# Where the rounded weights of a projection's first tile are kept, in a hybrid decoder step

## The chip, the cores and the metric

The kernel runs on one core of one Trainium2 chip. The metric is the device time of one execution in microseconds (us), the median over the runs shown.

## The reference, cut to what matters

One decoder layer works on 520 token columns (512 prompt positions and 8 samples) of width 1024. It opens and closes with half a gated feed-forward network; between the two stand a convolution group and an attention group with their projections.

```python
def half_ffn(x, g, w1, w3, w2):            # w1, w3: 1024 x 2816, w2: 2816 x 1024
    h = rmsnorm(x, g)
    return x + 0.5 * ((jax.nn.silu(h @ w1) * (h @ w3)) @ w2)

def trunk_layer(x, ffn1, mixw, ffn2, past):
    x = half_ffn(x, *ffn1)
    ...                                     # norm, w_in, convolution and attention, w_out
    x = half_ffn(x, *ffn2)
```

`h @ w1` and `h @ w3` are called the first projection here, and the product with `w2` the second projection.

## The kernel before

**Numbers in two parts.** Every float32 matrix is split into a rounded part `hi` (type float32r) and a rest `lo`. One product is three matmuls (`mm3`, lines 121 to 123): `hi` with the rounded activations, `hi` with their rest, `lo` with the rounded activations. Each has a 128x128 block of weights and 260 columns, half of the tokens. For the weights, `load_w` loads a block into a buffer `raw` (a ring of 4), ScalarE rounds it to `hi` (line 108), and VectorE subtracts to get `lo` (line 109). `hi` and `lo` come from two rings of 3 buffers with the tags `whi` and `wlo`.

**The feed-forward network** (`ffn`, run twice) cuts the 2816 hidden rows into 22 blocks of 128, and these into three stages by `CUTS = (0, 4, 14, 22)`. A stage makes its hidden blocks `hh`, `hl` and then calls `down`, which multiplies them with the rows of `w2` that belong to them and adds the result to `X`, in 8 tiles `m` of 128 output rows. The first stage makes its blocks one at a time. The second and the third make theirs two at a time (`pair`), each pair with two calls of `seven`, one for `w1` (results `a`) and one for `w3` (results `b`). `seven` gets four block products from seven products of half the depth (12 matmuls each) with sums of weights. Its operands are the two loaded weights `ha`, `hb` (with `la`, `lb`), which take two buffers each of the rings `whi` and `wlo`, and the three sums `hs`, `ls`, tiles of 12 blocks in a pool `su` with 2 buffers for each of the tags `hs` and `ls`. Their rounding is on lines 387 to 390. Lines 396 to 409 are the seven products, each followed by its copy or addition out of PSUM. In one accumulator (`px`) a later product goes on only after the copy of the earlier one (lines 397, 401, 405). A pair's last product is the seventh of `w3`; lines 330 and 334 to 338 then make the second hidden block of the pair out of it.

**The second projection.** `down` works on `k1 - k0` hidden blocks: 10 in the second stage, whose weights for one tile come as two loads of 5 blocks, and 8 in the third, one load of 8 blocks. A tile takes one PSUM buffer; `gemm` runs over the two halves of the columns and in each over the hidden blocks.

**Order.** The program order gives priorities. A planner with a timing model turns it, when the kernel is built, into a fixed order for each engine: an instruction whose operands the planner takes for ready can be put ahead of an earlier one that is not. On the chip each engine works through its list in that order. Loads are issued on the queue of SP in the order of their lists too.

**The transitions.** The text calls the passage from the pairs to `down` in the second stage the *first transition*, and in the third stage the *second transition*; there is one of each in both networks, four in all. At a transition the ring `whi` goes like this: the last pair's `w1` has two buffers; its `w3` takes the third for `ha`, and for `hb` the buffer that `ha` of `w1` gives back. The loads of `down` follow: the next buffer is free when the last product with `hb` of `w1` is done, the one after it when the product with `ha` of `w3` is done, and the third only when the pair's last product is done.

Of the kernel before, what the change touches and what calls it, by code (L numbers as in the profile page):

```python
# [8 lines left out]
F32R = mybir.dt.float32r  # L9
# [4 lines left out]
P = 128  # L14
# [6 lines left out]
KD = D // P  # L21
KF = DFF // P
# [16 lines left out]
CUTS = (0, 4, 14, 22)  # L39
# [7 lines left out]
def halves(t):  # L47
    return t.rearrange("p (h n) -> p h n", h=2)
# [3 lines left out]
def tile_step(ctx: ExitStack, tc: tile.TileContext, xT, w0, w1a, w3a, w2a, w_in, w_out, w1b, w3b, w2b,  # L52
# [6 lines left out]
    wp = ctx.enter_context(tc.tile_pool(name="wp", bufs=3))  # L59
# [13 lines left out]
    def preload():  # L73

        tc.keep_in_program_order(A.preload_act_table_set("natural_log_exp_and_others"))
# [4 lines left out]
    def PE_last():  # L80
        return [i for i in nc.cur_bb.bb.instructions if i.engine == mybir.EngineType.PE][-1]

    def keep_warm(n, ps):

        for _ in range(n):
            PE.matmul(ps[:, :P], lhsT=ones, rhs=ones, start=True, stop=True)
# [5 lines left out]
    loads = [0]  # L92
    EVERY = 5

    def load_w(src, n, cuts=None, then=None):
        raw = wp.tile([P, n, P], F32, name="raw", tag="raw", bufs=4)
        hi = wp.tile([P, n, P], F32R, name="hi", tag="whi")
        lo = wp.tile([P, n, P], F32R, name="lo", tag="wlo")
        if cuts:
            for c in cuts:  # L100
                SP.dma_start(raw[:, c], src[:, c])
                V.tensor_copy(hi[:, c], raw[:, c])
                V.tensor_tensor(lo[:, c], raw[:, c], hi[:, c].bitcast(F32), ALU.subtract)
                if c is cuts[0]:
                    then()
            return hi, lo
        load(raw, src)
        A.activation(hi, raw, AF.Copy)  # L108
        V.tensor_tensor(lo, raw, hi.bitcast(F32), ALU.subtract)  # L109
        return hi, lo  # L110

    def load(raw, src):
        d = SP.dma_start(raw, src)
        loads[0] += 1
        if side and loads[0] > 8 and loads[0] % EVERY == 0:
            with tc.issue_after(d.ins):
                side.pop(0)()
# [7 lines left out]
    def gemm(ps, parts, xh, xl, hs=(0, 1), of=None):  # L125

        ks = [(hi[:, i], lo[:, i], k0 + i) for hi, lo, k0, n in parts for i in range(n)]
        for h in hs:
            c = slice(h * TH, (h + 1) * TH)
            for i in range(*(of or (0, len(ks)))):  # L130
                hi, lo, k = ks[i]
                mm3(ps[:, h, :TH], hi, lo, xh[k][:, c], xl[k][:, c], i == 0, i == len(ks) - 1)
# [92 lines left out]
    def ffn(i, w1, w3, w2, g, psum, finish=None):  # L225
        turn, more = [0], []

        def psum_tile():
            turn[0] += 1
            pools = [(p, "m4") for p in more] + [(psM, "mm"), (psM, "mm"), (psum, "m3")]  # L230
            pool, tag = pools[(turn[0] - 1) % len(pools)]
            return pool.tile([P, 2, 512], F32, name="ps", tag=tag)

        Hh, Hl = [None] * KF, [None] * KF

        def hidden(m):
            at = m - max(c for c in CUTS if c <= m)
            pool = hids[at >= CUTS[1]]
            Hh[m] = pool.tile([P, T], F32R, name=f"hh{at}", tag=f"hh{at}")
            Hl[m] = pool.tile([P, T], F32R, name=f"hl{at}", tag=f"hl{at}")  # L240
            return Hh[m], Hl[m]

        with ExitStack() as st, ExitStack() as sx:
# [4 lines left out]
            with tc.tile_pool(name=f"xa{i}", bufs=1, side="right", reuse_waits="tile") as xa, \  # L248
# [23 lines left out]
                if early:  # L272

                    early, ws = [psum_tile() for _ in range(3)], early
                    for k in range(KD):
                        for e, ps in enumerate(early):
                            hi, lo = (t[:, 3 * (k % 2) + e] for t in ws[k // 2])
# [8 lines left out]
                for m in range(CUTS[1]):  # L286
# [3 lines left out]
                    for w, t in ((w1, a), (w3, b)):  # L290
# [5 lines left out]
                        hi, lo = load_w(w[m], KD)  # L296
# [19 lines left out]
            su = sx.enter_context(tc.tile_pool(name=f"su{i}", bufs=2, side="right", reuse_waits="tile"))  # L316

            def pair(m):

                at, aw, bt = psum_tile(), psum_tile(), psum_tile()  # L320
                a = gu.tile([P, 4, TH], F32, name="a", tag="a", bufs=2)
                b = gu.tile([P, 4, TH], F32, name="b", tag="b")
                x = seven(su, w1, m, xs, at, aw[:, 0, :TH], a)
                A.activation(a[:, 0:2], a[:, 0:2], AF.Silu)
                A.activation(a[:, 3], a[:, 3], AF.Silu, scale=-1.0)
                A.activation(a[:, 2], x, AF.Silu, scale=-1.0)
                x = seven(su, w3, m, xs, bt, aw[:, 1, :TH], b)
                V.tensor_tensor(b[:, 0:2], b[:, 0:2], a[:, 0:2], ALU.mult)
                V.tensor_tensor(b[:, 3], b[:, 3], a[:, 3], ALU.mult)
                V.tensor_tensor(b[:, 2], x, a[:, 2], ALU.mult)  # L330
                for r, sign in ((0, 1.0), (1, -1.0)):
                    hh, hl = (halves(t) for t in hidden(m + r))
                    of = b[:, 2 * r:2 * r + 2]
                    A.activation(hh, of, AF.Copy, scale=sign)
                    if r:
                        V.scalar_tensor_tensor(hl, of, sign, hh.bitcast(F32), ALU.mult, ALU.subtract)
                    else:
                        V.tensor_tensor(hl, of, hh.bitcast(F32), ALU.subtract)

            for c0, c1 in zip(CUTS[1:], CUTS[2:]):  # L340
                for m in range(c0, c1, 2):
                    pair(m)
                if c1 < KF:
                    down(w2, c0, c1, Hh, Hl, psum_tile)
            preload()
            sx.close()
            more.clear()
            down(w2, CUTS[-2], KF, Hh, Hl, psum_tile, finish)

    def x_sums(pool, tmp, name, col, k):  # L350

# [57 lines left out]
        V.tensor_tensor(out[:, 1], pw, out[:, 1], ALU.add)  # L409
        return px  # L410

    def down(w2, k0, k1, Hh, Hl, psum_tile, finish=None, ms=range(KD)):

        n = k1 - k0 if k1 - k0 <= KD else (k1 - k0) // 2

        def parts(m):
            return [load_w(w2[m, :, k:k + n], n) + (k, n) for k in range(k0, k1, n)]

        def update(m, ps, h):
            c = slice(h * TH, (h + 1) * TH)  # L420
            V.scalar_tensor_tensor(X[m][:, c], ps[:, h, :TH], 0.5, X[m][:, c], ALU.mult, ALU.add)

        def whole(m):
            ws = parts(m)
            ps = psum_tile()
            gemm(ps, ws, Hh, Hl)
            V.scalar_tensor_tensor(halves(X[m]), ps[:, :, :TH], 0.5, halves(X[m]), ALU.mult, ALU.add)
            if finish:
                finish(m, None)

        for m in ms[:-2] if finish else ms:
            whole(m)
        if not finish:
            return
        ws = [parts(m) for m in range(KD - 2, KD)]
        for h in range(2):
            for m in range(KD - 2, KD - 1):
                ps = psum_tile()
                gemm(ps, ws[m - KD + 2], Hh, Hl, [h])
                update(m, ps, h)  # L440
                finish(m, h)
            ps = psum_tile()
            if not h:
                gemm(ps, ws[-1], Hh, Hl, [0])
                update(KD - 1, ps, 0)
                give = finish(KD - 1, 0)
                continue
            gemm(ps, ws[-1], Hh, Hl, [1], (0, SPLIT))
            with tc.issue_after(tc.keep_in_program_order(give()).ins):
                gemm(ps, ws[-1], Hh, Hl, [1], (SPLIT, k1 - k0))  # L450
            idle = psum_tile()[:, 0]
            with tc.issue_after(PE_last()):
                keep_warm(4, idle)
            update(KD - 1, ps, 1)
            give = finish(KD - 1, 1)
            with tc.issue_after(PE_last()):
                keep_warm(4, idle)
            give()
# [357 lines left out]
    with tc.tile_pool(name="psB", bufs=1, space=PSUM, reuse_waits="tile") as psB, ExitStack() as st_f:  # L816
# [28 lines left out]
        def give(h, ps, r):  # L845

            fp, c = part["p"], slice(h * TH, (h + 1) * TH)
            both = [ps, part["ps"].tile([P, 512], F32, name="nps0", tag="n0")] if h else [ps]
            for p in both:
                mm = spread(p, r, TF, [(t, 0, TF) for t in range(4)])  # L850
            y = fp.tile([P, KD, TH], F32, name="yf", tag=f"yf{h}")
            rs = fp.tile([P, TH], F32, name="rs", tag=f"rs{h}")
            A.activation(rs, both[-1][:, :TH], AF.Copy)
            for ks in ((0,), (1, 2), (3, 4), (6, 7), (5,)):
                for k in ks:
                    if k > 5:
                        G.tensor_tensor(y[:, k], rs, X[k][:, c], ALU.mult)
                    else:
                        V.tensor_tensor(y[:, k], ps[:, :TH], X[k][:, c], ALU.mult)
                ks = slice(ks[0], ks[-1] + 1)  # L860
                SP.dma_start(yT[:, ks, c], y[:, ks])
            return mm

        ffn(1, w1b, w3b, w2b, GV["ffn2"], psB, finish)


# [96 lines left out]
```

## Time and profile before

| what | value |
|---|---|
| runs, median (lowest to highest) | 1001.39 us (1000.5 to 1004.54) |
| profiled execution, its own time | 1001.53 us |
| span of its trace, first to last instruction | 999.7 us |
| mean granted TensorE clock | 0.996 of full speed |

Sums are made against the 1001.53 us of the profiled execution. It lies 0.14 us above the median. The span leaves out 1.83 us of that time, which lie before and after the first and last instruction. The profile lists per engine when each instruction started and how long it took; `PE` is TensorE's matmuls, `PEld` its loads of weights, `DVE` VectorE, `ACT` ScalarE, `SPq` the queue that issues loads. "L108" is line 108 of the kernel.

### The profile page before, as it was taken

To read this page: it belongs to the slowest core of one execution; us is meant where nothing else is said; L and a number is where in the kernel's file an instruction comes from. 1 tells how busy PE (TensorE), PEld (TensorE's weight loads), DVE (VectorE), ACT (ScalarE), POOL (GpSimd) and SP (SyncE) were. 2 spreads that over 40 slices of the span, in tenths; PEclk is the share of its full clock that TensorE was granted. 3 is DMA by queue.
4 is the path that set the end of the run, shared out by engine and by line. 5 is a ranking of instruction groups with operands and counts; after the bars stand their busy time and mean duration, and the time that the engine had idled before them with its cause. 6 is when DMAs were issued, how large, how long until landed. Compare 5 with 4: busy or idle time off the path is not lost.

```text
span 999.7 us, 19200 instructions
## 1 busy us (share of the span) xinstructions
PE 977.4 (98%) x7897; PEld 955.6 (96%) x7897; DVE 719.6 (72%) x1153; ACT 519.9 (52%) x941; POOL 69.7 (7%) x89
## 2 busy tenths in 40 slices
PE   8999999999999999999999999999999999999997
PEld 8999999999999999999999899999999999999997
DVE  7889987336886446667788899769988634788432
ACT  5536665324665446667566555435656422565442
POOL 1000000000000131112022210000000000000022
PEclk9999999999999999999999999999999999999998
DMA  7344343445444444243146565325443233333302
GB/s 243 110 137 164 133 147 123 163 138 173 145 147 130 165 157 149 89 145 138 65 152 228 197 225 191 108 94 179 149 147 127 80 93 104 106 107 106 106 22 86
DMA packets 37912, 136.62 MB, mean 137 GB/s; under 512 B 5760, under 2 KB 8512, under 8 KB 37312
## 3 DMA queue, kind: packets, MB, share of 16 engines
q1 hardware_dynamic: 37824, 135.39, 39.9%
q8 instruction: 62, 1.02, 0.4%
q14 instruction: 26, 0.21, 0.1%
HBM read 131.07 MB, written 37.82 MB: 169 GB/s over the span
## 4 chain that ended last, share of the span: by engine, by line
PE 78%; DVE 11%; DMA 5%; issue 3%; ACT 2%; POOL 1%; SPq 0%; POOLq 0%; DVEq 0%; ACTq 0%
PE ps L121 24%; PE ps L123 24%; PE ps L122 24%; DVE lo L390 2%; DMA raw<-in_w3a 2%; PE s L589 1%; DMA raw<-in_w1a 1%; DVE ls L390 1%; DVE lo L109 1%; DMA raw<-in_w1b 1%; DVE raw L377 1%; PE pt L610 1%; DVE ws L378 1%; DVE ws L376 1%; DVE ws L375 1%
## 5 line engine op out<-in xcount | busy, mean ns | idle before, releaser
L108 ACT ACTIVATE hi<-raw 128x1024 fp32r<-128x1024 f32 (+3 forms) x136 | 119.0, 878 | 208.3 <-PE ps L122 162.7
L121 PE MATMUL ps<-hh,hi 128*128 128x260 f32 x704 | 198.4, 284 | 3.4 <-ACT hi L108 1.4
L123 PE MATMUL ps<-hh,lo 128*128 128x260 f32 x704 | 198.8, 284 | 1.2 <-DVE lo L109 1.2
L122 PE MATMUL ps<-hl,hi 128*128 128x260 f32 x704 | 198.2, 282 | 0.1
L109 DVE TENSOR_TENSOR lo<-raw,hi 128x1024 fp32r<-128x1024 f32 (+3 forms) x136 | 138.6, 1020 | 76.3 <-ACT hi L108 75.0
L121 PEld LDWEIGHTS ps<-hh,hi 128*128 128x128 f32 x704 | 132.3, 189 | 4.9 <-ACT hi L108 1.8
L123 PEld LDWEIGHTS ps<-hh,lo 128*128 128x128 f32 x704 | 132.2, 188 | 2.1 <-DVE lo L109 1.6
L122 PEld LDWEIGHTS ps<-hl,hi 128*128 128x128 f32 x704 | 132.6, 188 | 0.4 <-DVE hl L305 0.3
L121 PE MATMUL ps<-mh,hi 128*128 128x260 f32 x384 | 110.1, 287 | 1.7 <-DVE q L518 1.1
L123 PE MATMUL ps<-mh,lo 128*128 128x260 f32 x384 | 109.4, 285 | 0.2 <-DVE u L643 0.2
L122 PE MATMUL ps<-ml,hi 128*128 128x260 f32 x384 | 109.3, 285 | 0.0
L389 ACT ACTIVATE hi<-raw 128x512 fp32r<-128x512 f32 x144 | 82.9, 622 | 37.2 <-PE ps L122 27.9
L390 DVE TENSOR_TENSOR lo<-raw,hi 128x1024 fp32r<-128x1024 f32 x72 | 87.8, 1219 | 7.2 <-ACT hi L389 6.9
L123 PE MATMUL ps<-f1sh,lo 128*128 128x260 f32 x288 | 81.6, 285 | 1.8 <-DVE lo L390 1.7
L121 PE MATMUL ps<-f0sh,hi 128*128 128x260 f32 x288 | 81.8, 284 | 1.4 <-ACT a L405 1.0
L121 PE MATMUL ps<-f1sh,hi 128*128 128x260 f32 x288 | 81.5, 283 | 0.7 <-ACT a L405 0.5
L123 PE MATMUL ps<-f0sh,lo 128*128 128x260 f32 x288 | 81.3, 285 | 0.7 <-DVE lo L390 0.6
L122 PE MATMUL ps<-f0sl,hi 128*128 128x260 f32 x288 | 81.2, 282 | 0.0
L122 PE MATMUL ps<-f1sl,hi 128*128 128x260 f32 x288 | 81.1, 282 | 0.0
L144 POOL TENSOR_TENSOR acc<-acc,sq 128x520 f32<-128x520 f32 (+1 forms) x19 | 28.9, 1523 | 741.4 <-ACT sq L143 737.5
L121 PEld LDWEIGHTS ps<-mh,hi 128*128 128x128 f32 x384 | 72.4, 189 | 2.8 <-issue 1.8
L122 PEld LDWEIGHTS ps<-ml,hi 128*128 128x128 f32 x384 | 72.4, 188 | 1.1 <-issue 0.7
(278 smaller groups left out, 2664.5 us busy)
## 6 DMA issues: line engine op xcount, KB each, us to landing
out_cko<-in_ck SPq DMA_DIRECT2D x16, 1023.0 KB, 6.8
out_cvo<-in_cv SPq DMA_DIRECT2D x16, 1023.0 KB, 6.8
raw<-in_w_in SPq DMA_DIRECT2D x24, 512.0 KB, 3.3
raw<-in_w1b SPq DMA_DIRECT2D x22, 512.0 KB, 3.3
raw<-in_w3b SPq DMA_DIRECT2D x22, 512.0 KB, 3.3
raw<-in_w3a SPq DMA_DIRECT2D x21, 512.0 KB, 3.3
raw<-in_w1a SPq DMA_DIRECT2D x20, 512.0 KB, 3.3
raw<-in_w2a SPq DMA_DIRECT2D x16, 320.0 KB, 2.9
```

What stands on the lines that cost most here:

```text
L108: A.activation(hi, raw, AF.Copy)
L109: V.tensor_tensor(lo, raw, hi.bitcast(F32), ALU.subtract)
L121: PE.matmul(out, lhsT=hi, rhs=xh, start=start, stop=False, skip_group_check=more)
L122: PE.matmul(out, lhsT=hi, rhs=xl, start=False, stop=False, skip_group_check=more)
L123: PE.matmul(out, lhsT=lo, rhs=xh, start=False, stop=stop, skip_group_check=more)
L144: eng.tensor_tensor(dst[:, c], dst[:, c], sq[:, c], ALU.add)
L375: V.tensor_tensor(s[:, 0], rb[:, :KQ], rb[:, KQ:], ALU.add)
L376: V.tensor_tensor(s[:, 1], s[:, 0], ra[:, :KQ], ALU.add)
L377: V.tensor_tensor(rb[:, :KQ], rb[:, :KQ], ra[:, :KQ], ALU.add)
L378: V.tensor_tensor(s[:, 2], s[:, 1], ra[:, KQ:], ALU.add)
L389: A.activation(h[:, c:c + KQ], f[:, c:c + KQ], AF.Copy)
L390: V.tensor_tensor(l, f, h.bitcast(F32), ALU.subtract)
```

## The change

After the pairs of the second and third stage, the weights of the first tile (`m = 0`) of the second projection are loaded and rounded by a call of their own, and into other buffers: a tile of 12 blocks from the tags `hs` and `ls` of the pool `su` instead of buffers of the rings `whi` and `wlo`. `down` then takes these for `m = 0` and the rings for the other seven tiles. In the third stage the call stands ahead of the load of the activation table (`preload`) and of the closing of the pools; before, the loads of `m = 0` stood behind both.

```diff
-    def load_w(src, n, cuts=None, then=None):
+    def load_w(src, n, cuts=None, then=None, room=None):
         raw = wp.tile([P, n, P], F32, name="raw", tag="raw", bufs=4)
-        hi = wp.tile([P, n, P], F32R, name="hi", tag="whi")
-        lo = wp.tile([P, n, P], F32R, name="lo", tag="wlo")
+        hi, lo = room or (wp.tile([P, n, P], F32R, name=x, tag=f"w{x}") for x in ("hi", "lo"))
...
                 for m in range(c0, c1, 2):
                     pair(m)
+                room = [su.tile([P, 12, P], F32R, name=x, tag=x) for x in ("hs", "ls")]
+                first = down_weights(w2, c0, c1, 0, room)
                 if c1 < KF:
-                    down(w2, c0, c1, Hh, Hl, psum_tile)
+                    down(w2, c0, c1, Hh, Hl, psum_tile, first=first)
             preload()
             sx.close()
             more.clear()
-            down(w2, CUTS[-2], KF, Hh, Hl, psum_tile, finish)
+            down(w2, CUTS[-2], KF, Hh, Hl, psum_tile, finish, first=first)
...
-    def down(w2, k0, k1, Hh, Hl, psum_tile, finish=None, ms=range(KD)):
+    def down_weights(w2, k0, k1, m, room=None):
 
         n = k1 - k0 if k1 - k0 <= KD else (k1 - k0) // 2
+        return [tuple(load_w(w2[m, :, k:k + n], n, room=room and [t[:, k - k0:k - k0 + n] for t in room])) + (k, n)
+                for k in range(k0, k1, n)]
+
+    def down(w2, k0, k1, Hh, Hl, psum_tile, finish=None, ms=range(KD), first=None):
 
         def parts(m):
-            return [load_w(w2[m, :, k:k + n], n) + (k, n) for k in range(k0, k1, n)]
+            return first if first and not m else down_weights(w2, k0, k1, m)
```

## Rows read from the trace of the kernel before

**Rows 1.** The page: the busy time, share of the span and number of instructions of each engine, and the shares of the chain that ended last.

```profile
PE 977.4 (98%) x7897; PEld 955.6 (96%) x7897; DVE 719.6 (72%) x1153; ACT 519.9 (52%) x941; POOL 69.7 (7%) x89
...
PE 78%; DVE 11%; DMA 5%; issue 3%; ACT 2%; POOL 1%; SPq 0%; POOLq 0%; DVEq 0%; ACTq 0%
```

**Rows 2.** The waits of TensorE over the whole span: line waited for, us in total, times, longest.

```profile
PE ps L123 <- DVE lo L109: 2.6, 4, 1.0
...
PE ps L121 <- ACT hi L108: 1.4, 2, 0.7
...
PE ps L121 <- DVE b L330: 1.0, 2, 0.5
```

**Rows 3.** Stretches of the first network: the stretch and its length, then busy us and number of instructions of PE, PEld, DVE, ACT and POOL, the granted TensorE clock, the share of the DMA engines, GB/s. The first two are around and behind the first transition, the third is inside and after the last `down`.

```profile
188.00:196.00 8.00, 7.27 (x57) 6.71 (x56) 3.16 (x5) 2.55 (x4) 0.00 (x0) 1.00 0.15 43
196.00:229.00 33.00, 33.00 (x277) 33.00 (x276) 10.68 (x15) 6.86 (x10) 0.00 (x0) 1.00 0.51 170
...
345.00:385.00 40.00, 40.00 (x336) 40.00 (x335) 19.15 (x27) 16.28 (x23) 10.43 (x8) 1.00 0.40 141
```

**Rows 4.** TensorE's instructions in order of time at the first transition of the first network: start, duration, engine, line, output and inputs, and in brackets the idle time ahead and what ended it. The first row is the end of the pair's last product.

```profile
187.97 0.28 PE L123 MATMUL ps<-f0sh,lo 128*128 128x260 f32 x1
188.96 0.39 PE L121 MATMUL ps<-hh,hi 128*128 128x260 f32 x1 [0.71 <-ACT hi L108]
189.19 0.28 PE L122 MATMUL ps<-hl,hi 128*128 128x260 f32 x1
189.48 0.38 PE L121 MATMUL ps<-hh,hi 128*128 128x260 f32 x1
189.82 0.39 PE L123 MATMUL ps<-hh,lo 128*128 128x260 f32 x1
```

**Rows 5.** ScalarE and VectorE at the same place, in order of time for each: the first three roundings of weights of `down` (line 108), the rounding of the pair's second hidden block (line 334), the rest of the third rounding (line 109) and that of the hidden block (line 336).

```profile
180.43 0.74 ACT L108 ACTIVATE hi<-raw 128x640 fp32r<-128x640 f32 x1 [0.93 <-PE ps L122]
...
181.87 0.74 ACT L108 ACTIVATE hi<-raw 128x640 fp32r<-128x640 f32 x1 [0.43 <-PE ps L122]
...
188.17 0.74 ACT L108 ACTIVATE hi<-raw 128x640 fp32r<-128x640 f32 x1 [2.39 <-PE ps L122]
188.81 0.62 ACT L334 ACTIVATE hh<-b 128x520 fp32r<-128x520 f32 x1
...
188.94 0.83 DVE L109 TENSOR_TENSOR lo<-raw,hi 128x640 fp32r<-128x640 f32 x1 [0.23 <-ACT hi L108]
189.68 0.69 DVE L336 SCALAR_TENSOR_TENSOR hl<-b,hh 128x520 fp32r<-128x520 f32 x1
```

**Rows 6.** TensorE's instructions at the second transition of the first network: three places where the next start is late.

```profile
322.78 0.28 PE L122 MATMUL ps<-hl,hi 128*128 128x260 f32 x1
323.67 0.39 PE L123 MATMUL ps<-hh,lo 128*128 128x260 f32 x1 [0.61 <-DVE lo L109]
...
327.38 0.28 PE L123 MATMUL ps<-hh,lo 128*128 128x260 f32 x1
327.77 0.39 PE L121 MATMUL ps<-f0sh,hi 128*128 128x260 f32 x1
...
329.19 0.28 PE L123 MATMUL ps<-f0sh,lo 128*128 128x260 f32 x1
330.00 0.39 PE L121 MATMUL ps<-hh,hi 128*128 128x260 f32 x1 [0.52 <-DVE b L330]
```

**Rows 7.** ScalarE and VectorE at the second transition: the first rounding of `down` (lines 108 and 109), the copy out of `px` (line 405), the rest of the pair's first hidden block (line 338) and the multiplication that frees the last PSUM buffer of the pair (line 330).

```profile
321.29 1.06 ACT L108 ACTIVATE hi<-raw 128x1024 fp32r<-128x1024 f32 x1 [0.93 <-PE ps L122]
...
327.33 0.39 ACT L405 ACTIVATE b<-ps 128x260 f32<-128x260 f32 x1 [0.97 <-PE ps L123]
...
322.38 1.23 DVE L109 TENSOR_TENSOR lo<-raw,hi 128x1024 fp32r<-128x1024 f32 x1 [1.56 <-ACT hi L108]
...
326.40 0.70 DVE L338 TENSOR_TENSOR hl<-b,hh 128x520 fp32r<-128x520 f32 x1 [0.70 <-ACT hh L334]
...
329.51 0.43 DVE L330 TENSOR_TENSOR b<-ps,a 128x260 f32<-128x260 f32 x1 [0.87 <-PE ps L123]
```

**Rows 8.** TensorE at the two transitions of the second network: the rows that answer to the first two of rows 4 and of rows 6.

```profile
800.69 0.28 PE L123 MATMUL ps<-f1sh,lo 128*128 128x260 f32 x1
801.68 0.39 PE L121 MATMUL ps<-hh,hi 128*128 128x260 f32 x1 [0.71 <-ACT hi L108]
...
934.82 0.28 PE L122 MATMUL ps<-hl,hi 128*128 128x260 f32 x1
935.71 0.39 PE L123 MATMUL ps<-hh,lo 128*128 128x260 f32 x1 [0.61 <-DVE lo L109]
```

**Rows 9.** Inside the last pair ahead of each transition, by start: the loads of `w2` issued ahead of the first transition, the last matmul that reads the sums of `w1` (line 123 with `ls`), then VectorE's rest of `ha` of `w3` (line 390) and the first matmul that reads it; the last two again for the second transition.

```profile
159.30 15.89 SPq L113 DMA_DIRECT2D raw<-in_w2a  x4
...
168.72 0.29 PE L123 MATMUL ps<-f0sh,ls 128*128 128x260 f32 x1
...
171.53 1.23 DVE L390 TENSOR_TENSOR lo<-raw,hi 128x1024 fp32r<-128x1024 f32 x1 [0.63 <-ACT hi L389]
...
173.38 0.28 PE L123 MATMUL ps<-f0sh,lo 128*128 128x260 f32 x1
...
312.40 1.23 DVE L390 TENSOR_TENSOR lo<-raw,hi 128x1024 fp32r<-128x1024 f32 x1 [0.63 <-ACT hi L389]
...
314.25 0.28 PE L123 MATMUL ps<-f0sh,lo 128*128 128x260 f32 x1
```

## The prediction

> **What bounds the kernel now.** The page comes first [rows 1]: TensorE is busy 98% of the span and holds 78% of the chain that ended last; VectorE, at 72%, holds 11%. What counts is then where TensorE waits. In the list of its waits [rows 2] the reader sees that the projection's weights (lines 108 and 109) are behind 1.4 and 2.6 us of idle time, a few waits of under 1 us each, and line 330 behind 1.0 us. The stretches tell where these are not: from 196 to 229 us, inside the second projection, TensorE is busy all 33.00 us [rows 3], 277 matmuls, so 33.00 / 277 = 0.119 us from one start to the next. From 345 to 385 us it is the same, 336 in 40.00 us. From 188 to 196 us there are 57 where 8 / 0.119 = 67 would fit. The gaps belong to the transitions. So the timelines of the transitions come last, and every gap is measured from start to start, less 0.119, because the matmuls overlap.
>
> First transition, first network [rows 4]: after the pair's last product TensorE starts again 0.99 us later, so 0.87 us are lost, and "ACT hi L108" ended them. Then 189.19 to 189.48 and 189.48 to 189.82 lose another 0.17 and 0.22. Together 1.26 us; the ten missing matmuls, 10 x 0.119 = 1.2, say the same. The rounding waited for is the third of `down`: it starts at 188.17 [rows 5], just when the last product has given back the third ring buffer, ends at 188.91, and its rest runs from 188.94 to 189.77, after which line 123 starts at 189.82. The two roundings ahead of it, at 180.43 and 181.87, are tile 0's. Why is there nothing else to do? Tile 0 is held by the pair's second hidden block, whose `hh` is rounded at 188.81 and whose `hl` ends at 189.68 + 0.69 = 190.37; tile 1 has only these late weights.
>
> Second transition [rows 6]: one load is a whole tile, and tile 0's own is the late one. Its rounding starts at 321.29, its rest at 322.38, and ends at 323.61 [rows 7]; line 123 starts at 323.67 instead of 322.90, 0.77 us lost. Two further gaps have other causes: 327.38 to 327.77 (0.27 lost) is the copy of `px` at 327.33, and 329.19 to 330.00 (0.69 lost) is the PSUM buffer of tile 1, which line 330 gives back at 329.94. The second network repeats both transitions [rows 8]: 801.68 - 800.69 = 0.99 and 935.71 - 934.82 = 0.89.
>
> **The change part by part.** No instruction is added or removed. Per network three loads, three roundings and three rests move: tile 0's, two at the first transition and one at the second.
>
> *Ring buffers.* Each load of tiles 1 to 7 now takes a ring place that one of tile 0 had. At the first transition tile 1's two roundings get the places at 180.43 and 181.87, and with rests of 0.83 us each are done before 184, some 5 us ahead of 188.09, when the last product's stream ends. Tile 1 then has two halves, of which the first can run over nine of ten hidden blocks: 9 x 3 = 27 matmuls or 3.2 us, against the 190.37 - 188.09 = 2.3 us until the held block is there. The cover is enough, and the whole 1.26 us go. What now starts at 188.17 is tile 2's first rounding, wanted only after tile 1. Bounds: nothing, if the planner leaves the order as it is and the next wait takes over; 1.26 if all goes.
>
> *The second transition.* Tile 0's weights are ready before 322.65, and the 0.77 us go at their place. What is late next? Tile 0 goes on with the pair's first hidden block, whose `hl` is ready at 326.40 + 0.70 = 327.10 [rows 7] and whose third matmul started at 327.38 [rows 6], so its second at about 327.25: only some 0.15 us earlier are to be had there in the same order. After it the next product waited for the copy at 327.33, which comes earlier with the product it follows; this product can then start at about 327.35 instead of 327.77. Line 330 and tile 1's PSUM buffer follow it, 0.4 us earlier. So I take 0.4 of 0.77; the ends are 0 and 0.77.
>
> *Where the roundings go.* The room is the buffer of the sums of `w1`, whose last reader starts at 168.72 [rows 9], so it is free at 169.0, 11 us ahead of the old place, and the loads are issued from 159.30 on. The roundings then fall among those of the last pair's `w3`. The nearest rows for a price: the rest of `ha` ends at 171.53 + 1.23 = 172.76, and its first reader starts at 173.38; at the second transition 313.63 and 314.25. The slack is 0.62 us both times. One rest of 0.83 us in front costs 0.83 - 0.62 = 0.21, both cost 1.04, one of 1.23 costs 0.61. VectorE had 0.63 us of idle time just ahead of both rows, so part fits in; I take 0.2 us for the kernel as a whole, with bounds of zero and of the second rival's sum.
>
> *Loads, table load, pools.* SP issues the same loads in the same order; tile 0's `raw` come free earlier, and later loads with them. DMA engines are 15 to 51% busy in these stretches [rows 3]. The pools now close with tile 0's sums still in use, but nothing new there is written before tile 0 is added to `X`. I cost these at nothing; their cover is the 40.00 of 40.00 busy us after the second transition. Without it, a load would show as a new wait.
>
> [...]
>
> **Sum.** 2 networks x (1.26 + 0.4) = 3.3, less 0.2, is 3.1 us. 1001.53 - 3.1 = 998.4 us, and against the median, 1001.39, 3.0 us or 0.3% less.
>
> **The rivals.**
>
> *The next wait takes the place of the old.* At the first transition TensorE could run into the held block at 190.37 all the same, if its list keeps tile 0 ahead, or if both loads in one room tile are tracked as one. For it: the list is made with planned times, and in the gap [rows 4] it did not run tile 0's second half, though its weights were there. Against it: it did go on with tile 1, as soon as that had weights. Gain 0 to 1.5 us, time about 1000.6.
>
> *The earlier roundings hold up the last pair.* If the planner puts tile 0's in front of `w3`'s on both engines, then by the durations of their rows [rows 5, 7] the first transition costs 2 x 0.74 + 2 x 0.83 - 0.62 = 2.5 us and the second 1.06 + 1.23 - 0.62 = 1.7; two networks: 8.4, less 3.3: 5.1 us slower, 1006.6. On VectorE alone it is 2 x (1.04 + 0.61) = 3.3, which cancels the gain: 1001.5. So it decides from 0.83 us a transition beyond the slack. For it: the new place has only 0.62 us to spare. Against it: ScalarE is busy 52% and `w3`'s weights come first in the program. [...]
>
> *All gaps of the transitions go,* those of the copy and of line 330 too, since the new list fills them with tile 0's second half: 2 x (1.26 + 0.77 + 0.27 + 0.69) = 6.0, 995.5. Against it: the PSUM buffer is not touched by the change.
>
> *The planner orders other stages otherwise.* Attention has many short steps, whose order comes from the planned times. No row can price it; I give a few us either way, bounded by 5 or so, as much as the largest sum above.
>
> **How the numbers follow.** Chances: forecast 0.55, next wait 0.20, hold-up 0.10, all gaps 0.07, other stages 0.08. The likeliest gives 998.4. The range reaches up past the next wait and the cancelled gain to 1001.8, and down to 995.3, below all gaps gone; it leaves out most of a full hold-up and half of the last case, and some spread of the runs, about 2 in 10. A measurement of this kernel tells about 0.5% (5 us) from no change. Faster by more than that needs all gaps (0.04 of its 0.07), half of the last case (0.03) and 0.02 of the forecast: 0.09. Slower: 0.02 of the hold-up and 0.04 of the last: 0.06. The rest, 0.85, is within.
>
> **What would show it.** Right: no wait "ACT hi L108" over 0.5 us at the first transitions and no "DVE lo L109" at the second ones; three roundings per network on line 108 that start some 9 us earlier among the last pair's; tile 1's matmuls without a pause behind the last product. "DVE b L330" stays as a wait. Wrong: new waits on line 390 or on copies (lines 397 to 405) in the last pair, a pause until the held `hl` behind the last product, or a shift between 400 and 620 us that outweighs the 3 us.

## The result, and the profile after

The changed kernel takes 1014.83 us (median of 4 runs, 1010.43 to 1016.08), the kernel before 1001.39 us beside it (median of 3 runs, 1000.5 to 1004.54). Executions in a slow state, one of the kernel before with 1573.8 us and one in each of the first two experiments, are left out of the medians and ratios here. The ratio of the means is 1.012, with a 95% interval of 1.0096 to 1.0144. The change makes the kernel slower by 1.2%, where 998.4 us, or 0.3% less, had been forecast. The profiled execution took 1013.89 us with a span of 1012.1 us, 12.4 us more than the 999.7 before.

The page after, the line that answers to the first of [rows 1], and below it the groups of ScalarE in which tables of activation functions are loaded (line, engine, operation, count, then busy us and mean ns, and the idle time ahead):

```profile
PE 983.4 (97%) x7897; PEld 960.7 (95%) x7897; DVE 718.6 (71%) x1153; ACT 536.6 (53%) x955; POOL 69.3 (7%) x89
...
L75 ACT ACT_TABLE_LOAD x3 | 3.8, 1283 | 0.8 <-PEq L944 0.7
L182 ACT ACT_TABLE_LOAD x3 | 3.8, 1283 | 0.1
L183 ACT ACT_TABLE_LOAD x3 | 3.8, 1283 | 0.1
L149 ACT ACT_TABLE_LOAD x3 | 3.8, 1283 | 0.1
L150 ACT ACT_TABLE_LOAD x3 | 3.8, 1283 | 0.1
L300 ACT ACT_TABLE_LOAD x2 | 2.6, 1283 | 0.0
L323 ACT ACT_TABLE_LOAD x2 | 2.6, 1283 | 0.0
```

The same groups of the kernel before:

```profile
L75 ACT ACT_TABLE_LOAD x3 | 3.8, 1283 | 0.8 <-PEq L939 0.7
L301 ACT ACT_TABLE_LOAD x2 | 2.6, 1283 | 0.0
```

TensorE, VectorE and GpSimd have the same number of instructions as before [rows 1]; ScalarE has 955 instead of 941. The 14 that were added are table loads of 1.283 us each, 19 against 5. (Line numbers after are one to five off those before: line 107 is the old 108, line 391 the old 390; those of the experiments differ by a few too.) The new ones stand at the logarithms and exponentials of the norms (lines 149, 150, 182, 183) and at the Silu in a pair (line 323).

Where the time went is read from three updates of `X` on VectorE (line 427 or 421 before, 432 or 426 after): the last of the first network, the first of the second, and the last but one of the kernel. Before:

```profile
373.85 0.70 DVE L427 SCALAR_TENSOR_TENSOR X<-ps,X 128x520 f32<-128x520 f32 x1 [2.89 <-PE ps L123]
...
675.75 0.69 DVE L427 SCALAR_TENSOR_TENSOR X<-ps,X 128x520 f32<-128x520 f32 x1
...
984.09 0.43 DVE L421 SCALAR_TENSOR_TENSOR X<-ps,X 128x260 f32<-128x260 f32 x1 [0.31 <-PE ps L123]
```

After:

```profile
374.53 0.70 DVE L432 SCALAR_TENSOR_TENSOR X<-ps,X 128x520 f32<-128x520 f32 x1 [2.89 <-PE ps L122]
...
683.38 0.69 DVE L432 SCALAR_TENSOR_TENSOR X<-ps,X 128x520 f32<-128x520 f32 x1
...
992.23 0.43 DVE L426 SCALAR_TENSOR_TENSOR X<-ps,X 128x260 f32<-128x260 f32 x1 [0.31 <-PE ps L122]
```

The first network, with both of its transitions, costs 0.68 us more. Between the networks another 7.63 - 0.68 = 6.95 us are lost, in the second network 8.14 - 7.63 = 0.51, and behind this update 12.4 - 8.14 = 4.3. So over 11 of the 12.4 us are lost where no line of the change stands. TensorE's three longest waits between 380 and 660 us, first after, then before:

```profile
PE ps L120 <- DVE t L776: 2.8, 2, 2.3
PE ps L120 <- DVE q L523: 1.7, 1, 1.7
PE vt L556 <- DVE v L545: 1.1, 1, 1.1
```

```profile
PE ps L121 <- DVE q L518: 1.1, 1, 1.1
PE ps L121 <- DVE k L518: 0.6, 1, 0.6
PE ps L121 <- DVE t L771: 0.5, 1, 0.5
```

These are the users of the reciprocal roots that the norms deliver. ScalarE after, at the norm behind the first network, shows why they are late:

```profile
384.35 1.28 ACT L182 ACT_TABLE_LOAD   x1
385.65 0.64 ACT L182 ACTIVATE rbc<-rv 128x520 f32<-128x520 f32 x1
...
386.79 1.28 ACT L183 ACT_TABLE_LOAD   x1
388.09 0.64 ACT L183 ACTIVATE rbc<-rbc 128x520 f32<-128x520 f32 x1
```

A load stands ahead of the logarithm (line 182) and another ahead of the exponential (line 183), 2.57 us at one norm. Before, both functions ran at every norm without a load of their own (0 loads on their lines, 3 on line 75, which stand ahead of the norms). The two norms at the end have both loads too. At the last one, the logarithm and the load behind it:

```profile
1001.18 0.21 ACT L149 ACTIVATE rr<-rv 65x4 f32<-65x4 f32 x1
1001.40 1.28 ACT L150 ACT_TABLE_LOAD   x1
```

The waits are not the whole loss. By the full lists TensorE waits 6.7 us from 380 to 660 us after and 2.9 us before, 3.8 us more, where 6.95 us were lost. The rest goes with TensorE's granted clock, which in the changed kernel fell twice in this stretch and in the kernel before not at all. Two stretches of the changed kernel, in the columns of [rows 3]:

```profile
396.00:399.50 3.50, 3.15 (x14) 3.18 (x15) 3.23 (x5) 2.41 (x4) 1.12 (x1) 0.51 0.40 108
611.00:614.50 3.50, 3.50 (x19) 3.50 (x18) 2.18 (x4) 1.20 (x3) 0.00 (x0) 0.51 0.43 150
```

The second again in the kernel *Ring buffers, table load late* (see the experiments), which has the same loads at the norms:

```profile
611.00:614.50 3.50, 3.50 (x32) 3.50 (x31) 3.40 (x7) 2.14 (x4) 0.00 (x0) 1.00 0.47 150
```

At a granted clock of 0.51, 19 matmuls start where 32 start at 1.00; the 13 that are missing are worth 13 x 0.119 = 1.5 us. By the same two updates of `X` (374.18 and 681.72) that kernel, whose clock fell once here, lost 5.64 us, 1.3 us less than the changed kernel. So about 3 of the 6.95 us (an estimate: two falls at 1.3 to 1.5 us) are a lower clock behind the waits. Ahead of the first fall TensorE had waited 1.1 and 1.7 us (for `v` and `q`), ahead of the second 2.3 us (for `t`). The ring-buffer kernel has this last wait too and kept its clock, so why it falls at one place and not at another stays open. At the end of the kernel it was 0.84 from 990 to 1000 us, where the ring-buffer kernel had 1.00 and lost 3.5 us behind the third update instead of 4.3. The mean granted clock was 0.990 or 0.991 in all four runs of the changed kernel, against 0.996 before.

And why do the norms have loads of their own, with line 75's ahead of them? ScalarE before, behind the last pair of the first network, and after, inside that pair:

```profile
330.36 0.62 ACT L334 ACTIVATE hh<-b 128x520 fp32r<-128x520 f32 x1
331.00 1.28 ACT L75 ACT_TABLE_LOAD   x1
```

```profile
310.65 1.06 ACT L107 ACTIVATE hs<-raw 128x1024 fp32r<-128x1024 f32 x1 [2.12 <-PE ps L121]
311.73 1.28 ACT L75 ACT_TABLE_LOAD   x1
313.02 0.39 ACT L402 ACTIVATE a<-ps 128x260 f32<-128x260 f32 x1
...
317.29 1.28 ACT L323 ACT_TABLE_LOAD   x1
318.58 0.64 ACT L323 ACTIVATE a<-a 128x520 f32<-128x520 f32 x1
```

`preload` (line 75) is traced with `keep_in_program_order`. At the transitions shown here the load runs directly behind the one instruction that was traced just ahead of it on ScalarE, wherever the planner put that one. Before, that was the rounding of the pair's second hidden block, the last instruction of the pair there (330.36). After, it is the rounding of tile 0's weights. This runs at 310.65, inside the pair, and the table load follows at 311.73. At 317.29 a load for the pair's own Silu follows, and line 75 has no further load before the norms. At the norm at 384.35 both functions then have loads of their own; before, with line 75's load at 331.00, behind the pair's last Silu, neither has one. So in these runs it goes with the order of the two loads: with the Silu's last the norms have 12 loads (this kernel and *Ring buffers, table load late*), with line 75's last none (the kernel before and *Table load first*). The early load also holds up a copy out of `px` (line 402) for which TensorE waits; its timeline there:

```profile
311.88 0.28 PE L122 MATMUL ps<-f0sh,lo 128*128 128x260 f32 x1
313.46 0.39 PE L120 MATMUL ps<-f0sh,hi 128*128 128x260 f32 x1 [1.29 <-ACT a L402]
```

### The profile page after: what moved, and what is told of

It is laid out like the page before. It is cut to its first block, busy times and chain, and to the rows that moved or that the text cites. A ratio compares the mean times of both kernels' runs of the same rounds, so it can differ in the third digit from the quotient of the medians.

```text
span 1012.1 us, 19208 instructions
## 1 busy us (share of the span) xinstructions
PE 983.4 (97%) x7897; PEld 960.7 (95%) x7897; DVE 718.6 (71%) x1153; ACT 536.6 (53%) x955; POOL 69.3 (7%) x89
## 4 chain that ended last, share of the span: by engine, by line
PE 79%; DVE 9%; DMA 4%; issue 3%; ACT 2%; POOL 1%; SPq 0%; POOLq 0%; DVEq 0%; ACTq 0%
PE ps L120 25%; PE ps L122 25%; PE ps L121 24%; DVE lo L391 2%; PE s L594 1%; DMA raw<-in_w1a 1%; DMA raw<-in_w1b 1%; DVE lo L108 1%; PE pt L615 1%; DVE raw L378 1%; DVE ls L391 1%; DMA raw<-in_w3a 1%; DVE ws L377 1%; DMA X<-in_xT 1%; DVE ws L379 1%
## 5 line engine op out<-in xcount | busy, mean ns | idle before, releaser
L107 ACT ACTIVATE hi<-raw 128x1024 fp32r<-128x1024 f32 (+3 forms) x130 | 113.8, 878 | 193.9 <-PE ps L121 154.4
L108 DVE TENSOR_TENSOR lo<-raw,hi 128x1024 fp32r<-128x1024 f32 (+3 forms) x130 | 133.9, 1031 | 66.5 <-ACT hi L107 66.1
L120 PE MATMUL ps<-hh,hi 128*128 128x260 f32 x632 | 178.2, 284 | 1.5 <-ACT hh L304 0.9
L122 PE MATMUL ps<-hh,lo 128*128 128x260 f32 x632 | 178.4, 283 | 0.0
L121 PE MATMUL ps<-hl,hi 128*128 128x260 f32 x632 | 178.1, 283 | 0.1
L120 PEld LDWEIGHTS ps<-hh,hi 128*128 128x128 f32 x632 | 118.8, 189 | 2.5 <-ACT hh L304 1.1
L121 PEld LDWEIGHTS ps<-hl,hi 128*128 128x128 f32 x632 | 119.2, 189 | 0.4 <-DVE hl L304 0.3
L122 PEld LDWEIGHTS ps<-hh,lo 128*128 128x128 f32 x632 | 118.9, 188 | 0.1
```

The source lines that it names most:

```text
L120: PE.matmul(out, lhsT=hi, rhs=xh, start=start, stop=False, skip_group_check=more)
L121: PE.matmul(out, lhsT=hi, rhs=xl, start=False, stop=False, skip_group_check=more)
L122: PE.matmul(out, lhsT=lo, rhs=xh, start=False, stop=stop, skip_group_check=more)
```

## The experiments

All six kernels were timed beside the kernel before, in two series, each on one chip (median before 1002.14 us for the first four kernels, 1002.84 us for the last two). "The room" is the tile from `hs` and `ls` that takes tile 0's weights.

**Table load first.** In the changed kernel, the third stage's table load goes ahead of tile 0's weights:

```diff
                 for m in range(c0, c1, 2):
                     pair(m)
+                if c1 == KF:
+                    preload()
                 room = [su.tile([P, 12, P], F32R, name=x, tag=x) for x in ("hs", "ls")]
                 first = down_weights(w2, c0, c1, 0, room)
...
-            preload()
             sx.close()
```

> The changed kernel, with the load of the activation table (preload) of the third stage traced ahead of tile 0's weights instead of behind them; the room and everything else stay. Theory T (tables): in the changed kernel the table load was held only behind tile 0's rounding, so it ran inside the last pair and was undone by the pair's own Silu; 14 table loads of 1.28 us more follow, among them two around each logarithm and exponential of the norms. Then this kernel has 5 table loads as before, the 12 us are gone, and what is left is the room's own worth: 998 to 1002 us, no loss between 380 and 660 us or behind 985 us. Rival B (buffers): the room and the earlier roundings disturb the order of all stages; then it stays at 1008 to 1014 us, with any table loads.

Measured: 997.70 us, ratio 0.9964 (0.995 to 0.9978), just under the range of theory T. Against the changed kernel's own ratio of 1.012 that is 1.6% for the place of one line in the program. There are 5 table loads again. ScalarE at the end of the last pair, and TensorE at the one gap that is left at the second transition of the first network:

```profile
332.48 0.62 ACT L333 ACTIVATE hh<-b 128x520 fp32r<-128x520 f32 x1
333.12 1.28 ACT L75 ACT_TABLE_LOAD   x1
```

```profile
331.79 0.28 PE L122 MATMUL ps<-hh,lo 128*128 128x260 f32 x1
332.11 0.39 PE L120 MATMUL ps<-hh,hi 128*128 128x260 f32 x1
```

The table load is behind the last hidden block, as before the change. At the transition, 0.32 - 0.12 = 0.2 us are lost instead of 0.77 + 0.27 + 0.69 = 1.7 [rows 6], and from 296 to 350 us and from 905 to 960 us the list of TensorE's waits is empty. Theory T holds, rival B falls.

**Ring buffers, table load late.** The other way round: no room, only the trace order of the third stage changed.

```diff
                     down(w2, c0, c1, Hh, Hl, psum_tile)
+            first = down_weights(w2, CUTS[-2], KF, 0)
             preload()
...
-            down(w2, CUTS[-2], KF, Hh, Hl, psum_tile, finish)
+            down(w2, CUTS[-2], KF, Hh, Hl, psum_tile, finish, first=first)
```

> The other way round: ring buffers throughout as before, no room, the second stage as before; only in the third stage tile 0's weights are traced ahead of the load of the activation table. Theory T: 19 table loads, and a time of 1009 to 1015 us though no buffer is changed. Rival B: the time of before, 999 to 1004 us.

Measured: 1013.68 us, ratio 1.0121 (1.0101 to 1.0141), the whole loss of the change without its buffers. ScalarE at the second transition:

```profile
320.97 1.06 ACT L107 ACTIVATE hi<-raw 128x1024 fp32r<-128x1024 f32 x1 [0.93 <-PE ps L121]
322.05 1.28 ACT L75 ACT_TABLE_LOAD   x1
323.34 1.28 ACT L325 ACT_TABLE_LOAD   x1
```

Here the rounding runs at its old place, 10 us later than with the room, and still ahead of one Silu of the pair (line 325). That is enough: the Silu's own load follows line 75's 1.3 us later, and 19 loads stand in the trace. The gaps of the second transition stay: 0.6 us for line 108 (the old 109) and 0.5 us for line 329 (the old 330) in both networks. So what closes them in the kernel with the table load first is the room and not the trace order.

**No table load ahead of time.** The kernel before, without the third stage's `preload`:

```diff
-            preload()
             sx.close()
```

> The kernel before with the third stage's load of the activation table left out; the norms still get the tables they need, loaded where they stand, so the results are the same. Theory T: two table loads of 1.28 us around each of the six norms and none inside the last pairs, so that the share of the norms is seen by itself: 7 us between 380 and 660 us and 4 us behind 985 us, 1008 to 1013 us. Rival B, by which table loads are hidden beside TensorE: 1000 to 1004 us.

Measured: 1013.48 us, ratio 1.0119 (1.0102 to 1.0136), 0.5 us above the range of theory T and far from rival B. The loads are 15: two at each of six norms are new, the two of line 75 at the transitions are missing. TensorE's three longest waits between 380 and 660 us are those of the changed kernel, to the digit (2.8, 1.7 and 1.1 us), the first of them:

```profile
PE ps L121 <- DVE t L770: 2.8, 2, 2.3
```

So loads at the norms alone are enough for the whole loss. That the ratios are equal (1.012 and 1.0119) does not make the loads inside the last pairs free: the changed kernel has the room, which this one lacks and which is worth 0.36% with the table load first. That gain is missing in the changed kernel. The start at 313.46 comes 1.58 - 0.12 = 1.46 us late in the first network, and the one that answers to it in the second, at 933.01, as late; with the table load first neither wait is there. This is about what the room gains at the two second transitions.

**Room in the second stage only.** The first transitions with the room; the third stage as before.

```diff
+                if c1 < KF:
+                    room = [su.tile([P, 12, P], F32R, name=x, tag=x) for x in ("hs", "ls")]
+                    first = down_weights(w2, c0, c1, 0, room)
+                    down(w2, c0, c1, Hh, Hl, psum_tile, first=first)
+            first = None
             preload()
```

> The room only in the second stage (the first transitions); the third stage is as before. Theory T: 5 table loads. The changed kernel's first transitions lost 2.0 us of matmul starts in the first network against 2.2 before, and 3.3 against 2.6 in the second, so the room is worth nothing there: 1000 to 1003 us. Rival B: a large part of the loss stays, 1005 us or more.

Measured: 1003.06 us, ratio 1.0009 (0.9997 to 1.0021), and 5 table loads. The room gains nothing at the first transitions that these runs can tell; the 2 x 1.26 us of the prediction would be a ratio of 0.9975, outside the interval.

**Room in the third stage only.** The complement, with the table load ahead:

```diff
                 if c1 < KF:
                     down(w2, c0, c1, Hh, Hl, psum_tile)
+                    continue
+                preload()
+                room = [su.tile([P, 12, P], F32R, name=x, tag=x) for x in ("hs", "ls")]
+                first = down_weights(w2, c0, c1, 0, room)
```

> The room only in the third stage (the second transitions), with the table load traced ahead of it; the second stage as before. Theory T: 5 table loads; in the kernel with both rooms and the table load ahead, the second transitions lost 0.7 and 0.5 us of matmul starts against 2.3 and 2.1 before, so nearly all of its gain sits here: 996 to 1000 us. Rival C, that the gain needs the first transitions as well: 1000 us or more.

Measured: 997.83 us, ratio 0.9954 (0.9939 to 0.9969). The gain sits at the second transitions. By the gaps it should be 2 x (1.7 - 0.2) = 3.0 us; 0.46% of 1002.84 is 4.6, with an interval of 3.1 to 6.1. Whether more than the gaps went, no run here shows.

**Tile 1 held back.** Both rooms, the table load ahead, and in the second stage the matmuls of tiles 1 to 7 behind the last one of the pairs:

```diff
                 if c1 < KF:
-                    down(w2, c0, c1, Hh, Hl, psum_tile, first=first)
+                    last = PE_last()
+                    down(w2, c0, c1, Hh, Hl, psum_tile, first=first, ms=range(1))
+                    with tc.issue_after(last):
+                        down(w2, c0, c1, Hh, Hl, psum_tile, ms=range(1, KD))
```

> Both rooms, the table load ahead of the third stage's room, and in the second stage the matmuls of tiles 1 to 7 are held behind the last matmul of the last pair. Theory P (order): with the room the planner spent tile 1's matmuls between the pair's last products, so that behind the last product TensorE waited for a rounding again. Held back, tile 1 fills the 2.3 us there, the wait for the rounding goes, and each first transition loses some 1.2 us less: 995 to 997.5 us, about 2 us under the kernel with both rooms. Rival Q: the pair's last products wait for their copies without tile 1 between them, and the time stays at 997 to 1001 us.

Measured: 999.49 us, ratio 0.9963 (0.9944 to 0.9983), no different from both rooms without the hold (0.9964). TensorE's waits from 180 to 200 us, in this kernel, and below in the one with the table load first:

```profile
PE ps L120 <- DVE b L408: 0.5, 1, 0.5
PE ps L120 <- ACT b L410: 0.4, 1, 0.4
```

```profile
PE ps L120 <- DVE b L405: 0.5, 1, 0.5
PE ps L120 <- ACT hi L107: 0.2, 1, 0.2
```

The wait for the rounding is gone as theory P said, and a wait of 0.4 us for a copy of `px` has come instead. Rival Q holds: without tile 1 between them, the pair's last products wait for their copies.

## Why the prediction was wrong, point by point

**The step that failed** is "Loads, table load, pools", with the words "I cost these at nothing". The moved place of the call was seen, and its effect on the loads of weights was thought through, but not what the table load was tied to. The runs showed in its place 14 table loads more, 11.2 us lost at the norms (6.95 between the networks and 4.3 at the end, waits and lower clock together) and another 1.46 us in each last pair, which uses up the room's gain. "No instruction is added or removed" is wrong for the same reason. The cover that was named, 40.00 of 40.00 busy us, lies behind the second transition and ahead of the norms, where nothing was lost. The prediction asked who waits for tile 0's weights; it did not ask what is queued behind their rounding by the program itself. The trace of the kernel before had the price of one load, 1.283 us, in its five table loads, and the place behind line 334 at which two of them ran. Two loads at each of six norms and one more in each of two pairs make the 14; what part of their 18 us is paid no row could tell.

**The rivals** had the sign but not the mechanism. "The planner orders other stages otherwise" placed a loss between 400 and 620 us, and most of it fell there. But it is not the planner's order of short steps: without any table load ahead of time, and with no other change, the same waits stand there. "The next wait takes the place of the old" gave the right gain for the first transitions, none, though by neither of its two conditions: the wait is one for a rounding of the ring again. "The earlier roundings hold up the last pair" is seen at 313.46, but there the copy waited for the table load and not for a rounding: with the table load first, tile 0's rounding stands at the same place in the pair, and this wait is gone.

**The sum at the first transition** (1.26 us each) was wrong too: nothing was gained. TensorE after, in the first network, at the places where it is late:

```profile
186.34 0.28 PE L122 MATMUL ps<-f0sh,lo 128*128 128x260 f32 x1
187.14 0.39 PE L120 MATMUL ps<-f0sh,hi 128*128 128x260 f32 x1 [0.52 <-DVE b L404]
...
189.89 0.28 PE L120 MATMUL ps<-hh,hi 128*128 128x260 f32 x1
190.01 0.28 PE L120 MATMUL ps<-f0sh,hi 128*128 128x260 f32 x1
...
191.81 0.28 PE L122 MATMUL ps<-hh,lo 128*128 128x260 f32 x1
192.31 0.39 PE L120 MATMUL ps<-hh,hi 128*128 128x260 f32 x1 [0.23 <-ACT hi L107]
192.54 0.28 PE L121 MATMUL ps<-hl,hi 128*128 128x260 f32 x1
192.84 0.39 PE L120 MATMUL ps<-hh,hs 128*128 128x260 f32 x1
```

The gaps beyond 0.119 us are 0.68, 0.38 and 0.18, again 1.24 us, against 1.26 [rows 4]. The prediction kept tile 1's 27 matmuls in reserve until the pair's last product was done. In the new order tile 1, whose weights come from the ring (`hi`; tile 0's are `hs`), runs between the pair's products, as at 189.89, and the last product starts only at 190.01; behind the last one stands the third rounding of the ring, as before, now with tile 2's weights. Held back by hand, tile 1 does fill that place, and the copies take the time.

**The sum at the second transition** was too small: 0.4 us were forecast of 0.77, and 1.5 were gained, with the table load in its place. The gaps that the third rival named, those of the copy and of line 330, closed as well; that tile 0's second half fills them is likely, but was not tried by itself. With 0 and 1.5 for 1.26 and 0.4, the sum is 2 x 1.5 = 3.0 us: near the 3.1 forecast and the 3.6 measured with the table load first. That is luck, two errors that cancel.

**One buffer more:** at the second transition the buffer was what was missing (1.7 us of gaps went to 0.2 with the table load first), and the gap of the PSUM buffer closed too. At the first transition one buffer more closed nothing (1.26 us of gaps went to 1.24 in the first network).

## What to carry to other kernels

When new work is traced ahead of an instruction that is pinned behind the last one on its engine, the pin moves with it: look for what is held by such a tie before moving a call past it, and trace the pinned instruction first, as the first experiment does. Count the table loads of a profile before and after every change: here one misplaced load in each network went with 12 more at the norms (19 in all instead of 5) and 11.2 us, far from the line that was edited. Read the granted clock beside the waits: here it was 0.51 in two stretches behind waits of 1.1 to 2.3 us, about 3 us by the estimate above. Work that fills a gap is only in reserve if the order keeps it there; a planner that takes it earlier leaves the gap where it was.

## What the runs showed of the hardware

A table load took 1.283 us on every line, 19 times in one execution, and at the norm shown above ScalarE's next instruction started 0.02 us behind it. At the norms 12 loads are 15.4 us, and 6.95 + 4.3 = 11.2 us were lost there. Not all of this is time of the loads themselves: about 3 us of it are the stretches between the networks in which TensorE's granted clock was 0.51, behind the longer waits. So about half of the 15.4 us was paid directly (11.2 - 3 = 8.2, an estimate from the same rows). A logarithm followed by an exponential did not have the same number of loads everywhere. In the changed kernel there are two at each of six norms, the second right behind the logarithm at 1001.40, and the same 12 in the kernel without line 75's loads at the transitions. The changed kernel's first norm, at 29.26, has line 75's load of 0.73 ahead of it and none of its own. In the kernel before, with line 75's loads at 331.00 and 943.06, there is none at any norm.
